# A token-expert table made by matrix products of one-hot keys and stored plainly, in place of element-wise adds into a zeroed table

## The chip, the cores and the metric

The kernel runs on one core of a Trainium2 chip. The metric is the device time of one execution in microseconds (us). Engines are named as the profile names them: PE (TensorE, with PEld for its weight loads), DVE (VectorE), ACT (ScalarE), POOL (GpSimd) and SP (SyncE, which here only issues DMAs). Each engine works off its own queue in order. DMAs run on 16 DMA engines that all queues share.

## The reference

One layer of an encoder, for 1024 tokens of width 1024: a mixing half (attention and a linear recurrence) and a channel half, the PEER mixture of 128 x 128 = 16384 experts. The change touches only the channel half. For each token, 8 heads each choose 16 experts by a pair of keys (i, j), expert number 128 i + j, with softmax weights g:

```python
idx = jnp.take_along_axis(cand_idx, pos, axis=-1)      # 128 experts per token, 16 for each of 8 heads
g = jax.nn.softmax(best, axis=-1)
u = expert_u[idx]
v = expert_v[idx]
act = jax.nn.gelu(jnp.einsum('td,thkd->thk', xt, u))
return jnp.einsum('thk,thkd->td', (g * act).astype(xt.dtype), v)
```

Two heads of a token may choose the same expert; their weights then add up.

## The kernel before

Tokens go in 8 blocks of 128. Blocks 5, 6 and 7 (`GATHER`) fetch the rows of their chosen experts by indirect DMAs. Blocks 0 to 4 (`DENSE`, 640 tokens) are computed against all 16384 experts: 128 groups i of 128 experts each, group i being the experts 128 i + j. For that the weights g of a block stand in a table `d_G` in HBM, one number for each (expert, token), zero where the token did not choose the expert.

**The front.** `run` (L1384) calls `part(0)` and `part(1)`, each for 512 tokens: `attention`, `merge_a`, `lru`, `merge_b`, `ffn_in` (output projection, second norm, then 16 `query` and `score` steps that find each token's best 16 keys with `top16`). Work on the experts' choice is cut into steps in the list `self.steps`, and `pump` (L136) takes some of them at marked places of the stages (`self.rate`). `route(tb)` is the choice of one block, 18 steps on DVE; the places of block 4's routing and of the gathered blocks' are in the dense stage, those of blocks 0 to 3 in `part(1)`.

**The table.** `clear` (L1193) writes zeros over the table with 40 DMAs of 1 MB, one behind each weight load of `part(0)`. `route`'s last step puts the table's addresses `e` and weights `w` into tiles; `gates` (L1163) then issues, for each head and each of its 16 choices, one indirect DMA from POOL (L1174) that adds 128 numbers (one for each token) at 128 addresses in HBM. The 8 heads of a block wait for one another. That is 128 such DMAs a block, 512 for blocks 0 to 3 (`d_G[0]`, 512 tokens = `TE`) and 128 for block 4 (`LATE`, `d_G[1]`), which is routed in the dense stage. In the front they are issued by `pump` through a second rate (9 at most places).

**The dense stage.** `dense` (L1208) runs over the groups. `first(i)` is gelu(u_i h2) as `ps_A`, with operands in two parts (three matmuls for each product); `weigh(i)` multiplies by the table's rows (L1278); every second group `second` adds the product with v into `yac` as `ps_y`. `factors(g)` (L1264) loads the table's rows for two groups, tile `Gt`, one pair ahead; its DMA waits for all adds into that part of the table. Groups 0 to 19 (`KLATE`) work on 512 tokens, groups 20 to 127 on 640; the table part of block 4 is loaded from group 20 on. After the loop, a tail (L1347 on, `ps_Al` and `ps_yl`) computes groups 0 to 19 for block 4. Beside all this `pump` issues the gathers of blocks 5 to 7 (`g_u`, `g_v`: 768 indirect DMAs of 512 KB), first their routing at two steps a place (`FAST`), then at a rate worked out from the number of steps.

The order on each engine comes from a scheduler that takes instructions by their place in the program as their inputs become ready by its own estimate; a tile with a tag has `bufs` buffers and its next use waits for the release of an earlier one.

Of the kernel before, what the change touches and what calls it, by code (L numbers as in the profile page):

```python
# [25 lines left out]
LATE = tuple(b for b in DENSE if b >= S // 256)  # L26
TE = TD - 128 * len(LATE)
KLATE = 20 if LATE else 0
# [26 lines left out]
class Slices:  # L55
# [5 lines left out]
    def tile(self, shape, dt, name):  # L61
        n = int(np.prod(shape[1:]))
        if self.at + n > 1024:
            self.big, self.at = self.pool.tile([128, 1024], F32, tag="t4", bufs=11, name="small"), 0
# [17 lines left out]
class Builder:  # L82
    def __init__(self, ctx, tc, I, out, dbg=None, stop=None):
# [8 lines left out]
        self.rate = dict(unit=((1, 9), (2, 9)), ma=(3, 9), lru=(6, 9), mb=(2, 9), z=(4, 9), q=(2, 9))  # L92
        self.mark, self.heads_of, self.ahead = [], {}, []
        self.adds, self.turn, self.clears, self.due, self.last = {}, None, [], 0.0, None
# [15 lines left out]
    def weight(self, src, cols, scale=None, eng=None):  # L110
# [3 lines left out]
        self.last = nc.sync.dma_start(raw, src)  # L114
        if self.clears:
            self.clears.pop(0)()
# [19 lines left out]
    def pump(self, n, m=0.0):  # L136

        for _ in range(min(n, len(self.steps))):
            self.steps.pop(0)()
        self.due += m  # L140
        while self.due >= 1 and any(q and tb in self.ew for tb, q in self.adds.items()):
            tb = max((tb for tb, q in self.adds.items() if q and tb in self.ew),
                     key=lambda b: (b != self.turn, len(self.adds[b])))
            self.turn = tb
            self.adds[tb].pop(0)()
            self.due -= 1
        self.due = min(self.due, 1.0)
# [37 lines left out]
    def ada(self, g):  # L185
# [4 lines left out]
        def step(dk, h):  # L190
# [4 lines left out]
            w = fp.tile([128, 1024], F32, tag="t4", bufs=11, name="wada")  # L195
# [178 lines left out]
    def head(self, p):  # L374
# [6 lines left out]
        def load():  # L381
            s["x"] = []
            for i in range(4):
                x = fp.tile([128, 1024], F32, tag="t4", bufs=11, name="x")
# [3 lines left out]
        def start():  # L388
            junk = [fp.tile([128, 1024], F32, tag="t4", bufs=11, name="junk") for _ in range(2)]
# [82 lines left out]
    def part(self, p):  # L472
# [9 lines left out]
        if p == 0:  # L482
            self.clears = self.clear()
# [17 lines left out]
    def attention(self, p):  # L501
# [49 lines left out]
        def keys(h, blocks):  # L551
            t = heads.setdefault(h, {})
            if 0 in blocks:
                t["pq"], t["pk"] = self.psum([96, 512], "ps_qT"), self.psum([96, 512], "ps_kT")
                t["q"] = fp.tile([96, 512], F32, tag="t2", name="qT")
                t["k"] = fp.tile([96, 1024], F32, tag="t4", bufs=11, name="kT")
# [58 lines left out]
        for u in range(len(units) + lag + 1):  # L615
# [9 lines left out]
            self.pump(*self.rate["unit"][p])  # L625
# [5 lines left out]
    def softmax(self, p, i, qT, kT, scale):  # L631
# [3 lines left out]
        P = fp.tile([128, 1024], F32, tag="t4", bufs=11, name="P")  # L635
# [54 lines left out]
    def lru(self, p, hs, gb):  # L690
# [7 lines left out]
        def gate(g):  # L698
            t = grp[g] = [fp.tile([128, G, 512], F32, tag="t4", bufs=11, name=nm) for nm in ("ge", "rr", "uu", "bx")]
# [57 lines left out]
        for g in range(8 // G):  # L757
# [5 lines left out]
            self.pump(*self.rate["lru"])  # L763
# [4 lines left out]
        self.pump(*self.rate["lru"])  # L768
# [4 lines left out]
    def merge_a(self, p, hs, attn):  # L773
# [3 lines left out]
        for m in range(8):  # L777
# [9 lines left out]
            self.pump(*self.rate["ma"])  # L787
# [15 lines left out]
    def merge_b(self, p, gb, rec, yf):  # L803
        nc, I, fp = self.nc, self.I, self.fp
        for m in range(8):
# [9 lines left out]
            self.pump(*self.rate["mb"])  # L815
# [12 lines left out]
    def ffn_in(self, p, ys):  # L828
# [3 lines left out]
        for i in range(4):  # L832
            x = fp.tile([128, 1024], F32, tag="t4", bufs=11, name="x1")
# [7 lines left out]
        for cq in range(4):  # L841
# [13 lines left out]
            self.pump(*self.rate["z"])  # L855
# [30 lines left out]
        for i in range(4):  # L886
            if p * 4 + i in DENSE:
                late = p * 4 + i in LATE
                d = DENSE.index(p * 4 + i) * 128 - late * TE
                for j, t in enumerate(h2):  # L890
                    nc.sync.dma_start(self.d_h2T[late][j // 2, :, (j % 2) * 4:(j % 2) * 4 + 4, d:d + 128],
# [5 lines left out]
        st = fp.tile([128, 4, 16, 16], F32, tag="t4", bufs=11, name="st")  # L897
        it = fp.tile([128, 4, 16, 16], U32, tag="t4", bufs=11, name="it")
# [23 lines left out]
        late = [i for i in range(4) if p * 4 + i in GATHER or p * 4 + i in LATE]  # L922
# [5 lines left out]
        for c in range(17):  # L928
# [9 lines left out]
            self.pump(*self.rate["q"])  # L938
# [19 lines left out]
    def route(self, tb):  # L958

        nc = self.nc  # L960
        late = tb in GATHER or tb in LATE
# [20 lines left out]
        def start():  # L982

            if late:
                sit = self.gv([128, 2, 256], F32, "sit")
                self.after((nc.gpsimd if tb in LATE else nc.sync).dma_start(sit, self.d_st[tb]), self.mark)
# [53 lines left out]
        def end():  # L1040
# [15 lines left out]
            else:  # L1056
                pool = self.gp if late else self.fp
                w = pool.tile([128, 128], F32, tag="l_w", bufs=1 if late else TE // 128, name="g_w")
                e = pool.tile([128, 128], I32, tag="l_e", bufs=1 if late else TE // 128, name="g_e")
                nc.vector.tensor_copy(w, W2)  # L1060
                E = t["ij"][:, 0, :]
                nc.vector.scalar_tensor_tensor(E, E, 128.0, t["ij"][:, 1, :], op0=ALU.mult, op1=ALU.add)
                n = TD - TE if late else TE
                nc.vector.tensor_scalar(E, E, float(n), self.cols[:, 99:100], op0=ALU.mult, op1=ALU.add)
                nc.vector.tensor_scalar(e, E, float(DENSE.index(tb) * 128 - late * TE), None, op0=ALU.add)
                self.ew[tb] = e, w
# [96 lines left out]
    def gates(self, tb):  # L1163

        nc = self.nc
        late = tb in LATE
        G = self.d_G[late].rearrange("e (t o) -> (e t) o", o=1)

        def step(h):
            e, w = self.ew[tb]  # L1170
            prev, done = self.heads.get((late, tb), []), []
            others = [o for (l, b), v in self.heads.items() if l == late and b != tb for o in v]
            for s in range(h * 16, h * 16 + 16):
# [34 lines left out]
    def dense(self, da, db):  # L1208
# [119 lines left out]
        if not KLATE:  # L1328
            tokens_in(1, TE, TD)
# [162 lines left out]
```

## Time and profile before

| | us |
|---|---|
| median of 3 runs | 3929.08 (3922.1 to 3934.12) |
| the profiled execution | 3932.46 |
| its span, first to last instruction | 3930.7 |
| PE busy | 3208.3 (82%) |
| DVE busy | 2273.0 (58%) |
| ACT busy | 1105.3 (28%) |
| POOL busy | 2014.3 (51%) |
| DMA queues, share of 16 engines | 35.2% from POOL, 29.7% from SP |

Read by time, not by the shares: the program is a front (0 to about 1316 us), a dense stage (to 3849 us) and a tail. The slices in section 2 of the page show where an engine works; the view of stretches gives its busy time stage by stage; the view of waits says what a stage waited for. PE's clock is granted at 2.4 GHz (1.00) or 1.2 GHz (0.50).

### The profile page before, as it was taken

The numbers are of one execution on the slowest core, as the hardware profiler recorded it, in microseconds if no ns is written. First come the engines' busy times: TensorE is split into PE (matmuls) and PEld (weight loads), VectorE is DVE, ScalarE is ACT, GpSimd is POOL, SyncE is SP. The second block draws the span as 40 slices with busy tenths as digits, with TensorE's granted clock in tenths as the row PEclk, the third lists the DMA queues.
The fourth block names the chain that finished last, engine by engine and source line by source line (L and its number), as shares of the span: only waits on it lengthen the run. The fifth ranks groups of instructions, "written<-read, shape, count | busy, mean of one in ns | idle before, by whom it ended". The sixth has DMA issues, their size and how long they took to land. (4 is left out here: it accounts for less than half of the span.)

```text
span 3930.7 us, 46688 instructions
## 1 busy us (share of the span) xinstructions
PE 3208.3 (82%) x17310; PEld 2582.3 (66%) x17310; DVE 2273.0 (58%) x5192; ACT 1105.3 (28%) x1729; POOL 2014.3 (51%) x1439
## 2 busy tenths in 40 slices
PE   6899989699999500009907999999999999999998
PEld 4577777478688400007706888787888888787776
DVE  6436559883648400009806898677776777674443
ACT  4438343483823100004202222222222222222110
POOL 0000022388888888765774554555554555544440
PEclk9899999799999755559958999999999999999999
DMA  8577452135556322235426888999998999988887
GB/s 326 181 264 248 168 181 75 35 47 92 104 102 142 67 0 0 0 64 142 95 0 217 295 295 299 328 341 330 336 342 319 336 341 343 335 312 310 305 307 260
DMA packets 369212, 814.14 MB, mean 207 GB/s; under 512 B 118404, under 2 KB 157316, under 8 KB 365784
## 3 DMA queue, kind: packets, MB, share of 16 engines
q0 software_dynamic: 203120, 404.38, 35.2%
q1 hardware_dynamic: 165864, 406.78, 29.7%
q8 instruction: 136, 2.23, 0.2%
q14 instruction: 92, 0.75, 0.1%
HBM read 741.47 MB, written 69.55 MB: 206 GB/s over the span
## 5 line engine op out<-in xcount | busy, mean ns | idle before, releaser
L1174 POOL DMA_INDIRECT d_G<-g_w,g_e x640 | 1058.1, 1653 | 337.3 <-issue 203.3
L684 PE MATMUL ps_A<-dh,u 128*128 128x320 f32 (+1 forms) x1888 | 581.0, 321 | 557.0 <-ACT u L101 430.1
L684 PEld LDWEIGHTS ps_A<-dh,u 128*128 128x128 f32 x1888 | 356.6, 189 | 603.0 <-ACT u L101 432.4
L1095 POOL DMA_INDIRECT g_u<-in_expert_u,g_ei x384 | 470.4, 1225 | 401.6 <-PE ps_A L687 127.7
L1125 POOL DMA_INDIRECT g_v<-in_expert_v,g_eT x384 | 435.2, 1133 | 443.5 <-PE g_y L1139 137.4
L1101 DVE CUSTOM_DVE_ANT_0 g_u<-g_u,g_h 128x1024 f32<-128x1024 f32 x384 | 466.1, 1222 | 203.2 <-DMA g_u<-in_expert_u,g_ei 201.6
L685 PE MATMUL ps_A<-dh,u 128*128 128x320 f32 (+1 forms) x1888 | 576.0, 318 | 2.8 <-DMA dh<-d_h2T 2.8
L684 PE MATMUL ps_y<-v,w 128*128 128x512 f32 x1240 | 497.2, 401 | 23.4 <-ACT w L101 12.2
L685 PE MATMUL ps_y<-v,w 128*128 128x512 f32 x1240 | 488.0, 394 | 0.0
L101 ACT CAST v<-raw 128x1024 fp32r<-128x1024 f32 x128 | 134.4, 1050 | 1251.1 <-DMA raw<-in_expert_v 727.1
L1297 DVE TENSOR_TENSOR yac<-yac,ps_y 128x512 f32<-128x512 f32 x610 | 400.7, 683 | 72.6 <-PE ps_y L687 71.4
L687 PE MATMUL ps_y<-v,w 128*128 128x512 f32 x1240 | 391.1, 394 | 3.3 <-DVE w L102 1.4
L1278 DVE TENSOR_TENSOR a<-a,Gt 128x640 f32<-128x640 f32 (+1 forms) x128 | 102.6, 802 | 488.4 <-DMA Gt<-d_G 430.3
L685 PEld LDWEIGHTS ps_A<-dh,u 128*128 128x128 f32 x1888 | 356.9, 189 | 11.8 <-DMA dh<-d_h2T 3.4
L687 PE MATMUL ps_A<-dh,u 128*128 128x320 f32 (+1 forms) x1888 | 328.1, 316 | 0.0
L684 PEld LDWEIGHTS ps_y<-v,w 128*128 128x128 f32 x1240 | 233.9, 189 | 129.4 <-issue 28.5
L687 PEld LDWEIGHTS ps_A<-dh,u 128*128 128x128 f32 x1888 | 292.5, 188 | 6.3
L360 POOL TENSOR_TENSOR hT<-nfull,hT 128x512 fp32r<-128x512 f32 x8 | 10.2, 1288 | 548.7 <-ACT hT L359 548.5
L687 PEld LDWEIGHTS ps_y<-v,w 128*128 128x128 f32 x1240 | 234.3, 189 | 63.4 <-DVE w L102 13.5
L685 PEld LDWEIGHTS ps_y<-v,w 128*128 128x128 f32 x1240 | 234.5, 189 | 44.8
L102 DVE TENSOR_TENSOR v<-raw,v 128x1024 fp32r<-128x1024 f32 x128 | 156.3, 1221 | 165.7 <-ACT v L101 165.7
L102 DVE TENSOR_TENSOR whl<-wraw,whl 128x1024 fp32r<-128x1024 f32 (+2 forms) x136 | 155.7, 1146 | 155.7 <-ACT whl L101 155.6
(355 smaller groups left out, 5498.1 us busy)
## 6 DMA issues: line engine op xcount, KB each, us to landing
raw<-in_uT SPq DMA_DIRECT2D x128, 512.0 KB, 5.6
raw<-in_expert_v SPq DMA_DIRECT2D x128, 512.0 KB, 6.8
d_G<-zero SPq DMA_DIRECT2D x40, 1024.0 KB, 8.3
wraw<-in_w_in SPq DMA_DIRECT2D x64, 512.0 KB, 3.6
Gt<-d_G SPq DMA_DIRECT2D x64, 512.0 KB, 7.1
wada<-in_w_ada SPq DMA_DIRECT2D x32, 512.0 KB, 9.3
wraw<-in_w_query SPq DMA_DIRECT2D x32, 512.0 KB, 4.9
d_G<-g_w,g_e POOLq DMA_INDIRECT x640, 3.0
```

The source lines that it names most:

```text
L101: self.nc.scalar.copy(hi, src)
L102: (eng or self.nc.vector).tensor_tensor(lo, src, b32(hi), op=ALU.subtract)
L360: (eng or nc.vector).tensor_tensor(lo, full, b32(hi), op=ALU.subtract)
L684: nc.tensor.matmul(ps, lh, rh, start=(n == 0), stop=False)
L685: nc.tensor.matmul(ps, lh, rl, start=False, stop=False)
L687: st = nc.tensor.matmul(ps, ll, rh, start=False, stop=(n == len(terms) - 1))
L1095: st = nc.gpsimd.indirect_dma_start(out=u[:], out_offset=None, in_=I["expert_u"], in_offset=bass.IndirectOffsetOnAxis(ap=g["ei"][:, s:s + ...
L1101: nc.vector.tensor_tensor_reduce(out=u, in0=u, in1=g["h2"], scale=1.0, scalar=0.0, op0=ALU.mult, op1=ALU.add, accum_out=g["act"][:, s:s + 1])
L1125: st = nc.gpsimd.indirect_dma_start(out=v[:], out_offset=None, in_=I["expert_v"], in_offset=bass.IndirectOffsetOnAxis(ap=g["eT"][:, t:t + ...
L1174: st = nc.gpsimd.indirect_dma_start(out=G, out_offset=bass.IndirectOffsetOnAxis(ap=e[:, s:s + 1], axis=0), in_=w[:, s:s + 1], in_offset=No ...
L1278: nc.vector.tensor_tensor(a, a, Gs[g][:, m, :], op=ALU.mult)
L1297: nc.vector.tensor_tensor(yac[tb][:, ds], yac[tb][:, ds], ps, op=ALU.add)
```

## The change

`clear`, `gates`, the zero tile, `e` and `w`, the second rate of `pump` and the whole treatment of block 4 as a late block (`LATE`, `TE`, `KLATE`, the tail) go. `route(4)` moves into `part(1)`. The table becomes `d_G[c, j, i, t]`: token chunk c of `GC` = 32 tokens, then key j, key i and the token in its chunk. `table(tb)` makes a block's part of it in 33 steps. The first transposes the block's i, j and g (three 128 x 128 transposes on PE, one ACT copy `ch`), so that a token's 128 choices lie on the partitions. Each further step is for four tokens: `oneB` (one DVE instruction) compares the iota 0..127 with the choices' j, `oneA` (one DVE instruction for each token) compares it with i and multiplies by g; four fp32 matmuls `ps_G` give, for each token, the sum over the choices, a [j, i] matrix that is the table's part for that token; two ACT copies put it into the tiles `gs`, token innermost. After 8 steps two SP DMAs of 1 MB store 32 tokens; `gs` has two buffers, so the next 8 steps' copies wait for these stores. Where the program had `gates` now stands `table`: `pump` takes its steps from the one list, and what is left when `part(1)` is over runs before the dense stage. The tag `t4` has 9 buffers in place of 11.

```diff
-LATE = tuple(b for b in DENSE if b >= S // 256)
-TE = TD - 128 * len(LATE)
-KLATE = 20 if LATE else 0
+GC = 32
...
-        self.rate = dict(unit=((1, 9), (2, 9)), ma=(3, 9), lru=(6, 9), mb=(2, 9), z=(4, 9), q=(2, 9))
+        self.rate = dict(unit=(1, 2), ma=3, lru=6, mb=2, z=4, q=2)
...
-        self.last = nc.sync.dma_start(raw, src)
-        if self.clears:
-            self.clears.pop(0)()
+        nc.sync.dma_start(raw, src)
...
-                self.ew[tb] = e, w
+                self.chosen = t["ij"], W2
...
+    def table(self, tb):
+        nc, fp = self.nc, self.fp
+        t = {}
+        def start():
+            ij, W = self.chosen
+            pt = self.psum([128, 3, 128], "ps_ch")
+            for k, x in enumerate((ij[:, 0, :], ij[:, 1, :], W)):
+                nc.tensor.transpose(pt[:, k, :], x, self.ident)
+            t["ch"] = fp.tile([128, 3, 128], F32, tag="ch", bufs=1, name="ch")
+            nc.scalar.copy(t["ch"], pt)
+        def step(q):
+            ch = t["ch"]
+            if q % (GC // 4) == 0:
+                t["st"] = [fp.tile([128, 64, GC], F32, tag="gs", bufs=2, name="gs") for _ in range(2)]
+            B = fp.tile([128, 4, 128], F32, tag="t2", name="oneB")
+            A = fp.tile([128, 4, 128], F32, tag="t2", name="oneA")
+            iota = self.iota
+            nc.vector.tensor_tensor(B, iota[:, None, :].to_broadcast([128, 4, 128]),
+                                    ch[:, 1, q * 4:q * 4 + 4, None].to_broadcast([128, 4, 128]), op=ALU.is_equal)
+            for m in range(4):
+                n = q * 4 + m
+                nc.vector.tensor_scalar(A[:, m, :], iota, ch[:, 0, n:n + 1], ch[:, 2, n:n + 1], op0=ALU.is_equal,
+                                        op1=ALU.mult)
+            ps = self.psum([128, 4, 128], "ps_G")
+            for m in range(4):
+                nc.tensor.matmul(ps[:, m, :], B[:, m, :], A[:, m, :], start=True, stop=True)
+            k = q % (GC // 4) * 4
+            for m in range(2):
+                nc.scalar.copy(t["st"][m][:, :, k:k + 4].rearrange("p i t -> p t i"), ps[:, :, m * 64:(m + 1) * 64])
+            if q % (GC // 4) == GC // 4 - 1:
+                c = DENSE.index(tb) * (128 // GC) + q // (GC // 4)
+                for m in range(2):
+                    nc.sync.dma_start(self.d_G[c, :, m * 64:(m + 1) * 64, :], t["st"][m])
+        return [start] + [lambda q=q: step(q) for q in range(32)]
...
-        points = (128 * 2 + len(groups) * NB + KLATE) * RATE
+        points = (128 * 2 + len(groups) * NB) * RATE
...
         def factors(g):
...
-            Gs[g] = da.tile([128, hi - lo, n], F32, tag="G", bufs=2, name="Gt")
-            for k, (p0, p1) in enumerate(((0, TE), (TE, n))):
...
+            Gs[g] = da.tile([128, TD // GC, hi - lo, GC], F32, tag="G", bufs=2, name="Gt")
+            nc.sync.dma_start(Gs[g].rearrange("j c i t -> j c (i t)"),
+                              self.d_G[:, :, lo:hi, :].rearrange("c j i t -> j c (i t)"))
...
-        for k, tb in enumerate(LATE):
...
                 for tb in range(p * 4, p * 4 + 4):
-                    if tb in DENSE and tb not in LATE:
-                        self.steps += self.soon[tb] if tb in self.soon else self.route(tb)[0]
-                        self.adds[tb] = self.gates(tb)
-            self.pump(1 << 30, 1 << 30)
+                    if tb in DENSE:
+                        self.steps += (self.soon[tb] if tb in self.soon else self.route(tb)[0]) + self.table(tb)
+            self.pump(1 << 30)
...
-            for tb in LATE:
-                self.steps += self.route(tb)[0] + self.gates(tb)
```

PE's queue in `merge_a` of `part(1)`, between the two projections of one output chunk and those of the next. Before:

```order
L685 MATMUL ps_pa<-attnl,whl 128x512
L687 MATMUL ps_pa<-attnh,whl 128x512 x4
L684 MATMUL ps_ga<-hT,whl 128x512
L685 MATMUL ps_ga<-hT,whl 128x512
L684 MATMUL ps_ga<-hT,whl 128x512
```

The same place now:

```order
L670 MATMUL ps_pa<-attnl,whl 128x512
L672 MATMUL ps_pa<-attnh,whl 128x512 x4
L1169 MATMUL ps_G<-oneA,oneB 128x128 x9
L669 MATMUL ps_ga<-hT,whl 128x512
L1169 MATMUL ps_G<-oneA,oneB 128x128 x3
L670 MATMUL ps_ga<-hT,whl 128x512
```

Three steps' matmuls, 12, now stand between the projections, and the queue passes them only when DVE has made their one-hots. Counted over the whole queue, the 640 matmuls of `ps_G` stand so: 177 within `part(1)`'s attention, 79 in `merge_a`, 40 in `lru`, 88 in `merge_b`, and 256 from the query steps on.

DVE's queue where `part(1)` ends and the dense stage begins (`u` is the split of the first expert weights, `a` the first use of the table). Before:

```order
L951 MATCH_REPLACE wk<-st,sc 128x128
L102 TENSOR_TENSOR u<-raw,u 128x1024
L952 MAX st<-wk 128x8
L953 MAX_INDEX it<-st,wk 128x8
L102 TENSOR_TENSOR u<-raw,u 128x1024
L1278 TENSOR_TENSOR a<-a,Gt 128x512
```

Now, after 29 steps of the same two rows:

```order
L1161 TENSOR_TENSOR oneB<-cst,ch 128x512
L1165 TENSOR_SCALAR oneA<-cst,ch 128x128 x4
L1161 TENSOR_TENSOR oneB<-cst,ch 128x512
L1165 TENSOR_SCALAR oneA<-cst,ch 128x128 x4
L1161 TENSOR_TENSOR oneB<-cst,ch 128x512
L1165 TENSOR_SCALAR oneA<-cst,ch 128x128 x4
L99 TENSOR_TENSOR u<-raw,u 128x1024 x2
L99 TENSOR_TENSOR v<-raw,v 128x1024
L99 TENSOR_TENSOR u<-raw,u 128x1024
L1248 TENSOR_TENSOR a<-a,Gt 128x640
```

All 32 steps of block 4 stand at the end of the front, behind the last of its routing, and the split of the first `u` comes after them.

SP's queue at the same place. Before:

```order
L1241 DMA raw<-in_uT 128x1024
L1323 DMA dh_11528<-d_h2T_95 128x4x512
L1323 DMA dh_11529<-d_h2T_95 128x4x512
L1323 DMA dh_11537<-d_h2T_95 128x4x512
L1323 DMA dh_11531<-d_h2T_95 128x4x512
L1241 DMA raw<-in_uT 128x1024
L1268 DMA Gt<-d_G_97 128x2x512
L1241 DMA raw<-in_expert_v 128x1024
```

Now:

```order
L1292 DMA dh_13387<-d_h2T 128x2560
L1176 DMA d_G<-gs 128x2048 x2
L1216 DMA raw<-in_uT 128x1024
L1176 DMA d_G<-gs 128x2048 x6
L1216 DMA raw<-in_expert_v 128x1024
L1216 DMA raw<-in_uT 128x1024
L1239 DMA Gt<-d_G 128x20x64
L970 DMA sit<-d_st 128x512
L1239 DMA Gt<-d_G 128x20x64
```

The stores of block 4's table stand on the same queue as the dense stage's loads, ahead of the first `Gt`; and a `Gt` load is now 128 x 20 pieces of 64 numbers (256 bytes) where it was 128 x 2 pieces of 512 and later 128 x 2 more of 128.

## Rows read from the trace of the kernel before

**Rows 1.** The page's 40 slices of 98 us: busy tenths, PE's granted clock.

```profile
PE   6899989699999500009907999999999999999998
POOL 0000022388888888765774554555554555544440
PEclk9899999799999755559958999999999999999999
```

**Rows 2.** Waits, one line each: who waited for whom, us, times, longest.

```profile
DVE a L1278 <- DMA Gt<-d_G: 430.3, 1, 430.3
PE ps_A L684 <- DVE yac L1297: 125.6, 3, 124.6
```

**Rows 3.** Stretches: length, busy us of PE, PEld, DVE, ACT, POOL, clock, DMA share, GB/s.

```profile
726.00:887.00 161.00, 150.53 (x876) 111.31 (x877) 131.07 (x553) 117.12 (x257) 119.75 (x72) 0.90 0.29 39
887.00:1151.00 264.00, 257.05 (x1088) 204.98 (x1087) 124.97 (x161) 136.62 (x167) 224.35 (x131) 0.99 0.53 102
1211.50:1316.00 104.50, 102.84 (x516) 86.34 (x514) 100.82 (x494) 36.60 (x55) 88.94 (x52) 1.00 0.59 130
1333.00:1762.00 429.00, 0.49 (x3) 0.20 (x2) 2.73 (x4) 2.86 (x4) 340.57 (x223) 0.50 0.24 10
1762.00:1960.00 198.00, 194.69 (x842) 158.44 (x842) 185.76 (x517) 72.08 (x91) 129.41 (x69) 0.99 0.54 129
1960.00:2085.00 125.00, 0.37 (x3) 0.11 (x1) 1.98 (x3) 2.09 (x2) 92.01 (x60) 0.52 0.23 10
2085.00:3849.00 1764.00, 1738.51 (x10035) 1418.88 (x10036) 1230.12 (x1817) 382.76 (x546) 905.55 (x768) 0.99 0.89 318
3849.00:3931.00 82.00, 71.06 (x402) 50.96 (x401) 17.35 (x31) 5.54 (x20) 0.00 (x0) 0.97 0.77 281
```

**Rows 4.** The use of the table, by its line: durations, first and last start.

```profile
L1278 DVE TENSOR_TENSOR a<-a,Gt x128: 669/821/886, 1756.8 to 3833.0; 128x640 f32<-128x640 f32 x108, 128x512 f32<-128x512 f32 x20
```

**Rows 5.** Groups of instructions in the front, shapes apart: busy us, mean ns, idle before.

```profile
L736 DVE TENSOR_TENSOR bx<-ig,xc 128x512 f32<-128x512 f32 x16 | 11.0, 687 | 36.3 <-ACT ig L734 36.3
L661 DVE TENSOR_SCALAR P<-P,sm 128x128 f32<-128x128 f32 x8 | 2.3, 282 | 0.1
L588 ACT COPY PT<-ps_pT 128x256 f32<-128x256 f32 x16 | 6.0, 375 | 10.2 <-PE ps_pT L586 10.2
```

**Rows 6.** Order of time in the query steps, DVE and PE: start us, us, instruction.

```profile
1285.52 0.27 DVE L952 MAX8 st<-wk 128x8 f32<-128x128 f32 x1
1285.71 0.28 DVE L949 MAX8 st<-sc 128x8 f32<-128x128 f32 x1
1255.05 1.05 PE L915 MATMUL ps_sc<-sk,qrT 128*128 128x128 f32 x8
1255.86 0.48 PE L684 MATMUL ps_qr<-h2T,whl 128*128 128x512 f32 x1
```

**Rows 7.** The stretch 682 to 887, instructions on routing tiles alone (`rM`, then `eq`).

```profile
682.00:887.00 205.00, 0.00 (x0) 0.00 (x0) 47.58 (x276) 1.26 (x4) 0.87 0.26 42
682.00:887.00 205.00, 42.41 (x48) 0.87 0.26 42
```

**Rows 8.** DMA issues: KB each, median us from issue to landing.

```profile
Gt<-d_G SPq DMA_DIRECT2D x64, 512.0 KB, 7.1
d_hT<-hT SPq DMA_DIRECT2D x8, 1024.0 KB, 3.9
```

**Rows 9.** The stretch 2600 to 3500, instructions on `ps_A` alone, then on `ps_y`.

```profile
2600.00:3500.00 900.00, 403.55 (x2688) 395.71 (x2688) 46.44 (x112) 1.00 0.92 336
2600.00:3500.00 900.00, 402.69 (x1687) 311.25 (x1688) 181.39 (x280) 0.00 (x0) 1.00 0.92 336
```

**Rows 10.** DMA packets of one queue in 1288.2:1292, 1400:1700 and 2624.5:2625.

```profile
q1 hardware_dynamic: 144, 0.07, 6.0%
...
q0 software_dynamic: 22608, 0.09, 22.1%
...
q1 hardware_dynamic: 76, 0.16, 83.9%
```

More of the change, by code (lines that the diff above doesn't have):

```diff
@@ L134, in rsqrt, with pump @@
         return y
-    def pump(self, n, m=0.0):
+    def pump(self, n):
         for _ in range(min(n, len(self.steps))):
             self.steps.pop(0)()
[L140 to L147, printed above, removed]
     def show(self, name, ap):
@@ L624, in attention @@
                 mixes.pop(u - lag - 1)()
-            self.pump(*self.rate["unit"][p])
+            self.pump(self.rate["unit"][p])
         if p == 0:
@@ L762, in lru @@
                 scan(g - 1)
-            self.pump(*self.rate["lru"])
+            self.pump(self.rate["lru"])
         for m in range(G):
@@ L767, in lru @@
         scan(8 // G - 1)
-        self.pump(*self.rate["lru"])
+        self.pump(self.rate["lru"])
         if p == 1:
@@ L920, in score @@
                 self.top16(sc[:, i, :], w2, st[:, i, c, :], it[:, i, c, :])
-        late = [i for i in range(4) if p * 4 + i in GATHER or p * 4 + i in LATE]
+        late = [i for i in range(4) if p * 4 + i in GATHER]
         for i in range(4):
@@ L1160, in finish @@
         nc.sync.dma_start(self.out[tb * 128:(tb + 1) * 128, :], gr)
[L1163 to L1173, printed above, removed]
-                st = nc.gpsimd.indirect_dma_start(
-                    out=G, out_offset=bass.IndirectOffsetOnAxis(ap=e[:, s:s + 1], axis=0),
-                    in_=w[:, s:s + 1], in_offset=None, compute_op=ALU.add)
-                for o in done:
-                    self.tc.declare_no_dep(st.ins, o, reason="the experts of a head are distinct")
-                for o in others:
-                    self.tc.declare_no_dep(st.ins, o, reason="the columns of two blocks are distinct")
-                self.after(st, prev)
-                done.append(st.ins)
-            self.heads[late, tb] = done
-        return [lambda h=h: step(h) for h in range(8)]
+    def table(self, tb):
[32 more added lines that the diff above has]
+        return [start] + [lambda q=q: step(q) for q in range(32)]
@@ L1226, in pump @@
             self.mark = [st.ins]
-        def tokens(i):
-            return TE if i < KLATE else TD
         started = set()
@@ L1283, in second @@
             lo, hi = groups[g]
-            for tb in range(tokens(lo) // 128):
+            for tb in range(NB):
                 cs = slice(tb * 128, (tb + 1) * 128)
```

140 lines of the change are left out of this document (33 added, 107 removed).

## The prediction

> **What bounds the kernel now.** I read the slices first [rows 1]. POOL works from slice 6 on; PE is at 9 tenths nearly everywhere, but shows two holes, slices 15 to 18 and 21, with its clock at 0.5. The view of waits names them [rows 2]: DVE's first use of the table waits 430.3 us for the load `Gt`, and PE waits 124.6 us behind DVE at group 20, where block 4's part of the table is first used. Both loads wait for POOL's adds into HBM. The view of stretches confirms it [rows 3]: from 1333 to 1762 and from 1960 to 2085 PE works 0.5 and 0.4 us while POOL is busy. So 554 us are a wait for the way the table is made. Everywhere else the stages are full: in `merge_a`, `lru` and `merge_b` (887 to 1151) PE is busy 257.05 of 264 us, in the query steps (1211.5 to 1316) PE and DVE both about 101 of 104.5, in the dense stage PE 1738.51 of 1764 with DMA at 0.89. New work in the front therefore isn't free, and that is the sum to make.
>
> The program falls at one point: the first use of the table, `weigh(0)`, starts at 1756.8 [rows 4]. I work out when it starts now, and then what follows it (3930.7 - 1756.8 = 2173.9 us).
>
> **Price of a step of `table`** (four tokens, 160 steps in all). On DVE one instruction 128x512 and four 128x128 with two per-partition scalars; the nearest rows are 687 and 282 ns [rows 5], together 1.815 us, an upper end. Back to back, an instruction starts before the one ahead has ended (0.27 long, the next 0.19 later, [rows 6]), some 85 ns each: 1.39 us, which I take. On PE four fp32 matmuls 128x128: the same four in a score step (x8, two records for each) take 1.05 us, and the next matmul starts 0.81 after [rows 6]; I take 0.9 a step. On ACT two copies of 128x256 at 375 ns [rows 5]: 0.75.
>
> **Front.** Counted by PE's queue, 44 steps stand in the attention, 52 in `merge_a` to `merge_b`, 64 (blocks 3 and 4) from the query steps on.
> Attention: PE 150.5 + 44 x 0.9 = 190 us against 161 now, +29 if it filled every gap, +40 at today's idle 10.5 us. DVE would have 131 - 44 (the routing of two of the four blocks leaves: 47.58 + 42.41 us for four, [rows 7], so 22 a block) + 61 = 148, ACT 117 + 33: neither is the bound. +40, bounds 25 and 60 (each step at DVE's price).
> `merge_a` to `merge_b`: PE alone gives 52 x 0.9 = +47. PE meets the matmuls in queue order, three steps in a clump in `merge_a`, and waits if DVE is late; if it waited each time, 52 x 1.815 = +94. DVE's load is 125 + 44 + 72 = 241 us in a stretch of 311, so it is mostly in time: a third of the way, +62.
> `z` to the normalised transpose: +3.
> Query steps: DVE is the bound: 32 steps of block 3 are 45 us, half of block 4's routing 12: +58, bounds 54 and 70.
> Then everything that `pump` has left: the rest of block 4's routing, 14 us of chained DVE work, 32 steps (45 us, 58 at the upper price), the last copies, a store (1 MB lands in 3.9 us, [rows 8]) and the first `Gt` (7.1): 16 more. +75, bounds 62 (routing hidden) and 95 (58, and PE at its low clock because it idles, as in the holes of [rows 1]). Nothing can cover this: the dense stage needs the whole table.
> `weigh(0)`: 1316 (end of the query steps) + 40 + 62 + 3 + 58 + 75 = **1554**, 203 earlier than now; bounds 1504 and 1640.
>
> **Dense stage.** From 2173.9: the second hole goes, -125 [rows 2]. The tail of groups 0 to 19 for block 4, 82 us from 3849 on [rows 3], goes except for some 12 us of last sums and stores: -70. In its place 20 groups work on 640 tokens instead of 512: a group costs PE 403.55/56 = 7.21 us for `ps_A` and 402.69/56 = 7.19 for `ps_y` [rows 9], so a fifth of 14.4, 2.9 x 20 = +58. The clearing stores and POOL's adds cost nothing on the path outside the holes. The routing of blocks 5 to 7 stays in the first ten groups, where DVE was busy 185.76 of 198 us [rows 3] with 512 tokens; at 640 it is over full: +12.
> The load `Gt`: 16 + 16 pieces on each DMA engine before, 160 of 256 bytes now. Three prices of a piece are in the trace [rows 10] (busy share x time x 16 engines / packets): 512 bytes in 1288.2 to 1292 took 28 ns, 2048 bytes about 88, and an add of 4 bytes (a read and a write) 46.9. Before, a load cost 16 x 88 + 16 x 28.5 = 1.86 us of every engine. No row shows 256 bytes: half of 28.5 is 14 (2.3 us a load), the add's price is 47 (7.5 us). I take about 21, between the first two, since these too are plain reads: +1.5 us for each pair of groups. A pair takes 2 x 900/56 = 32.1 us with DMA at 0.92 [rows 9], so 2.5 us are free, and the load is one pair ahead. But more pieces take longer to get past the gathers' pieces (landing 15 to 28 us instead of 7.1, my estimate from five times the pieces), and weight loads stand behind on SP's queue. +20, bounds 0 and 165.
> Sum: 2173.9 - 125 - 70 + 58 + 12 + 20 = 2069. With `weigh(0)` at 1554 the span is 3623, and 1.8 us lie outside it: 3625 against 3932.46 of the profiled execution, -308. That execution is 3.4 above the median, so **3620**.
>
> The rows give 512 bytes 28 ns and 2048 bytes 88 [rows 10]: a piece costs nearly by its bytes. The Trainium skill (DMA: Bandwidth & Descriptors, Specifications) names 512 bytes as the least transfer for line rate, and the layout that this change gives the table is below that. By this rule a 256-byte piece would cost as much as one of 512, 4.6 us a load, 2.7 more than before; against 2.5 us free that adds some 10 us in all, which is within my +20. If it cost twice as much, it is the first rival. No run here shows pieces of 256 bytes.
>
> **Rivals.**
> *DMA becomes the bound of the dense stage.* At the add's 47 ns a load costs 5.6 us more, 3.1 over what is free, in some 54 pairs: +165 in place of +20, 3765. For it: DMA at 0.92, PE's queue without reserve, gathers and weights sharing the engines. Against: these are reads, and 512 bytes took 28 ns.
> *The steps run one after another.* If PE waits in full for the one-hots of each of the 96 steps that stand among PE's own work, each costs 1.815 + 1.05 = 2.87 us instead of the 102/96 = 1.06 taken: +173, 3790. For it: clumps of three steps in `merge_a`. Against: DVE's queue is free to run ahead by some buffers, and its load fits.
> *A light front.* Steps at the lower bounds everywhere (25 + 47 + 54 + 62, `weigh(0)` at 1504) and pieces that cost nothing: 3620 - 50 - 20 = 3550.
> *Slower than before.* It has one place: `Gt` in the dense stage, if a small piece is far dearer than I take. What I count as gained, 308 + 20 = 328 us, over 64 loads is 5.1 us each; with the 2.5 free and the 1.86 of now a load would have to keep every engine 9.5 us, 59 ns a piece. From there on the change loses; at 65 ns it is 3620 - 20 + 64 x (10.4 - 1.86 - 2.5) = 3985. The nearest row is 46.9, of an operation that does more.
> *It doesn't do what it says*: the dense stage still waits for the table, because SP's queue stores 20 MB of it just ahead. Of 16 x 1 MB for block 4 only the last pair is late; this is in the 16 us above.
>
> **How the numbers follow.** The forecast's case 0.65 (3570 to 3700), DMA as the bound 0.14, steps one after another 0.07, a light front 0.09, slower 0.04, and 0.01 for a cancellation near zero. Measured times of this kernel tell 0.3%, 12 us, from no change. The range reaches from the light front to the DMA rival: 3550 to 3770; left out are the serial steps, the slower case and the edges. Faster 0.95, same 0.01, slower 0.04.
>
> **What would show it.** The holes of [rows 1] gone, and `weigh(0)` near 1554; if it is there by 1500, the one-hots are cheaper than rows 5 and 6 say, if after 1640, PE waits for them. The instructions `oneB` and `oneA` sum to about 1.4 us a step, `ps_G` to 0.9. Query steps and what follows them last about 240 us. In the dense stage groups stand 16.1 us apart as now; with DMA as the bound the spacing rises to 17.6, the DMA share goes to 0.98 and PE's `ps_A` or DVE's `a` waits for weights or `Gt`. The tail `ps_Al` is gone, and the span ends some 12 us after the last group. The forecast fails if pieces cost over 40 ns, or if the 32 steps at the end of the front take over 100 us.

## The result

The changed kernel takes 3799.58 us (median of 4 runs, 3796.31 to 3811.1) against 3926.32 for the kernel before: a ratio of 0.968, with a 95% interval of 0.9654 to 0.9706. It is faster, as forecast, but by 127 us and not by the 308 of the sum, and the time lies above the whole range (3550 to 3770).

The page of the changed kernel, its slices (now 95 us each), for [rows 1]:

```profile
PE   6899989689988966569988999999999999999997
POOL 0000013000000000000144445555555555444400
PEclk8899999799999987779999999999999999999998
```

Both holes are gone, and so is nearly all of POOL's work in the front. In their place there is a shallow dip in slices 15 to 18: PE at 5 and 6 tenths, its clock at 0.7 to 0.8. The use of the table, for [rows 4] (line, count, durations in ns, first and last start):

```profile
L1248 DVE TENSOR_TENSOR a<-a,Gt x128: 794/821/887, 1735.1 to 3772.5; 128x640 f32<-128x640 f32 x128
```

`weigh(0)` starts at 1735.1; the forecast had 1554, the kernel before 1756.8. From there to the end are 3809.3 - 1735.1 = 2074 us; the forecast had 2069. So the whole miss, 181 us, lies ahead of the dense stage. The stretches of the changed kernel, for [rows 3] (length, busy PE, PEld, DVE, ACT, POOL, clock, DMA share, GB/s): attention, merges with the recurrence, query steps, what follows them, groups 0 to 19, the other groups, the end.

```profile
727.00:956.00 229.00, 197.21 (x1217) 152.85 (x1218) 172.65 (x643) 158.87 (x339) 0.00 (x0) 0.93 0.22 79
956.00:1300.00 344.00, 314.37 (x1506) 259.36 (x1505) 232.30 (x521) 192.93 (x278) 0.00 (x0) 0.96 0.34 117
1370.00:1641.00 271.00, 173.88 (x746) 149.12 (x745) 154.08 (x711) 64.71 (x110) 0.00 (x0) 0.79 0.18 62
1641.00:1735.00 94.00, 61.21 (x387) 54.69 (x387) 80.87 (x255) 43.04 (x81) 1.75 (x2) 0.85 0.57 210
1735.00:2024.00 289.00, 273.02 (x1489) 244.59 (x1488) 252.53 (x560) 84.50 (x119) 73.41 (x58) 0.98 0.65 207
2024.00:3772.00 1748.00, 1706.58 (x9880) 1390.95 (x9880) 1156.12 (x1686) 376.55 (x536) 813.57 (x710) 1.00 0.87 300
3772.00:3809.00 37.00, 13.93 (x60) 10.73 (x59) 20.03 (x22) 1.17 (x2) 0.00 (x0) 0.73 0.36 128
```

The query steps stand out. They took 104.5 us with PE and DVE both full [rows 3]; now they take 271, and neither engine is full: PE 174, DVE 154. An engine that is the bound is busy; here nobody is, so the two wait for each other. The view of waits over 1372 to 1641 says so:

```profile
PE ps_G L1169 <- DVE oneA L1165: 97.1, 21, 7.3
DVE st L933 <- ACT sc L901: 97.0, 12, 8.9
```

And the order of time shows one turn of it (start, us, what; in brackets the idle time before and who ended it):

```profile
1451.67 1.05 PE L899 MATMUL ps_sc<-sk,qrT 128*128 128x128 f32 x8
...
1453.30 0.59 ACT L901 COPY sc<-ps_sc 128x512 f32<-128x512 f32 x1
1453.92 0.49 DVE L933 MAX8 st<-sc 128x8 f32<-128x128 f32 x2 [8.47 <-ACT sc L901]
...
1458.14 0.34 DVE L1165 TENSOR_SCALAR oneA<-cst,ch 128x128 f32<-128x128 f32 x1
...
1458.63 4.13 PE L1169 MATMUL ps_G<-oneA,oneB 128*128 128x128 f32 x16 [5.90 <-DVE oneA L1165]
...
1462.41 0.77 PE L669 MATMUL ps_qr<-h2T,whl 128*128 128x512 f32 x1
...
1469.05 1.05 PE L899 MATMUL ps_sc<-sk,qrT 128*128 128x128 f32 x8
```

Read it as a ring. PE makes the scores (`ps_sc`, 1451.67). ACT copies them. DVE, idle for 8.47 us, starts the choice at 1453.92, and only when that is nearly done comes the one-hot that PE's next instruction needs (1458.14). PE, idle for 5.90 us, does two steps of the table, then the next projection `ps_qr` (1462.41), then the next scores (1469.05), for which DVE has begun to wait. One turn is 17.4 us: 2.3 to the scores' arrival, 4.7 to the one-hots, 3.8 of `ps_G`, 6.6 of projection. Sixteen turns are 278 us, and the stage lasts 271. Before, the same projection, scores and choice overlapped, 6.5 us for a query step.

### The profile page after: what moved, and what is told of

Same layout as the page of the kernel before. It is cut to its first block, busy times and chain, and to the rows that moved or that the text cites. A ratio compares the mean times of both kernels' runs of the same rounds, so it can differ in the third digit from the quotient of the medians.

```text
span 3809.3 us, 50002 instructions
## 1 busy us (share of the span) xinstructions
PE 3427.5 (90%) x18805; PEld 2810.2 (74%) x18805; DVE 2543.8 (67%) x5976; ACT 1271.9 (33%) x2054; POOL 938.1 (25%) x798
## 5 line engine op out<-in xcount | busy, mean ns | idle before, releaser
L669 PE MATMUL ps_A<-dh,u 128*128 128x320 f32 x2048 | 609.7, 311 | 5.2 <-DVE yac L1267 5.2
L1070 POOL DMA_INDIRECT g_u<-in_expert_u,g_ei x384 | 453.7, 1181 | 620.3 <-DMA raw<-in_uT 218.1
L670 PE MATMUL ps_A<-dh,u 128*128 128x320 f32 x2048 | 605.9, 309 | 0.0
L669 PE MATMUL ps_y<-v,w 128*128 128x512 f32 x1280 | 515.7, 403 | 49.5 <-DVE yac L1267 40.4
L670 PE MATMUL ps_y<-v,w 128*128 128x512 f32 x1280 | 504.4, 394 | 0.1
L1267 DVE TENSOR_TENSOR yac<-yac,ps_y 128x512 f32<-128x512 f32 x630 | 414.1, 682 | 95.5 <-PE ps_y L672 94.2
L669 PEld LDWEIGHTS ps_A<-dh,u 128*128 128x128 f32 x2048 | 385.3, 188 | 38.2 <-issue 20.1
L672 PE MATMUL ps_y<-v,w 128*128 128x512 f32 x1280 | 402.9, 394 | 2.2 <-DVE w L99 0.7
L670 PEld LDWEIGHTS ps_A<-dh,u 128*128 128x128 f32 x2048 | 385.5, 188 | 1.8
L1169 PE MATMUL ps_G<-oneA,oneB 128*128 128x128 f32 x1280 | 226.0, 329 | 160.1 <-DVE oneA L1165 148.3
L669 PEld LDWEIGHTS ps_y<-v,w 128*128 128x128 f32 x1280 | 242.4, 189 | 168.7 <-DVE yac L1267 64.6
L672 PE MATMUL ps_A<-dh,u 128*128 128x320 f32 x2048 | 343.2, 310 | 0.0
L1169 PEld LDWEIGHTS ps_G<-oneA,oneB 128*128 128x128 f32 x1280 | 202.0, 230 | 191.4 <-issue 123.2
L672 PEld LDWEIGHTS ps_A<-dh,u 128*128 128x128 f32 x2048 | 312.4, 189 | 0.0
L672 PEld LDWEIGHTS ps_y<-v,w 128*128 128x128 f32 x1280 | 242.3, 189 | 62.2 <-DVE w L99 10.0
L670 PEld LDWEIGHTS ps_y<-v,w 128*128 128x128 f32 x1280 | 242.6, 190 | 46.2 <-DVE v L99 0.5
L1172 ACT COPY gs<-ps_G 128x256 f32<-128x256 f32 x320 | 167.6, 641 | 219.5 <-PE ps_G L1169 193.9
```

Source lines behind the costliest of these rows:

```text
L669: nc.tensor.matmul(ps, lh, rh, start=(n == 0), stop=False)
L670: nc.tensor.matmul(ps, lh, rl, start=False, stop=False)
L672: st = nc.tensor.matmul(ps, ll, rh, start=False, stop=(n == len(terms) - 1))
L1070: st = nc.gpsimd.indirect_dma_start(out=u[:], out_offset=None, in_=I["expert_u"], in_offset=bass.IndirectOffsetOnAxis(ap=g["ei"][:, s:s + ...
L1169: nc.tensor.matmul(ps[:, m, :], B[:, m, :], A[:, m, :], start=True, stop=True)
L1172: nc.scalar.copy(t["st"][m][:, :, k:k + 4].rearrange("p i t -> p t i"), ps[:, :, m * 64:(m + 1) * 64])
```

## The experiments

Three questions: is it this ring; which link closes it; and what do the steps cost once it is open? The theory is that PE's `ps_G`, standing ahead of the next projection in PE's queue and reading one-hots that stand behind the choice in DVE's queue, closes the ring. Against it stood two rivals: that the steps are simply dear, wherever they stand; and that the ring closes through the split of the next query weights (`whl`), which also stands behind the one-hots on DVE.

**No steps in the query stage.**

```diff
-        self.rate = dict(unit=(1, 2), ma=3, lru=6, mb=2, z=4, q=2)
+        self.rate = dict(unit=(1, 2), ma=3, lru=6, mb=2, z=4, q=0)
```

> No step of the table is taken at the query steps' places; the 64 steps of blocks 3 and 4 and block 4's routing all run after them, and nothing else is changed. Theory (loop): in the changed kernel the query stage lasts 269 us, with DVE idle 97 us for the scores and PE idle 97 us for the one-hots, because PE's table matmuls stand ahead of the next projection and wait for one-hots that DVE makes only behind the choice from the last scores. Then the query stage falls back to 105 to 112 us, what follows it grows from 92 to about 92 + 32 x 1.63 + 12 = 156, the first use of the table comes at about 1637 and the time is about 3700. Rival (load): the steps cost the same wherever they stand, 5 us each in this part of the program; the time stays within 15 us of 3800.

Measured: 3690.73 us, ratio to the kernel before 0.9401 (0.9376 to 0.9427). Query stage and what follows it, in its stretches:

```profile
1358.60:1460.50 101.90, 101.90 (x514) 86.50 (x513) 100.28 (x483) 34.12 (x52) 0.00 (x0) 1.00 0.32 106
1460.50:1613.30 152.80, 94.36 (x622) 83.55 (x621) 140.97 (x494) 71.95 (x141) 1.75 (x2) 0.88 0.45 171
```

The stage is back at 102 us with PE full at 1.00, and 64 steps in a row behind it cost 153, with DVE busy 141 of them. The same work takes 110 us less for standing elsewhere. The rival "dear wherever they stand" is out.

**The matmuls two steps behind their one-hots.** Nothing is left out; a step now issues the matmuls, copies and stores of two steps before.

```diff
+        def mats(q):
+            A, B = t.pop(q)
...
+        def both(q):
+            if q >= 2:
+                mats(q - 2)
+            if q < 32:
+                step(q)
-        return [start] + [lambda q=q: step(q) for q in range(32)]
+        return [start] + [lambda q=q: both(q) for q in range(32 + 2)]
```

> The same instructions, but a step's four matmuls, copies and stores are issued two steps behind its one-hots. Theory (loop, closed by PE's table matmuls): PE finds the one-hots ready, the query stage falls from 269 to 165 to 185 us (DVE's 152 busy plus little), the time to about 3710; attention and the merges gain some 20 us as well. Rival 1 (loop, closed by the split of the next query weights, which stands behind the one-hots on DVE): the query stage stays above 230. Rival 2 (load): unchanged, 3800 within 15.

Measured: 3634.56 us, ratio 0.9241 (0.9225 to 0.9256). That is 165 us below the changed kernel, and the expected 3710 was 75 too high. Its attention, query stage and what follows that, by stretches:

```profile
722.90:911.40 188.50, 178.15 (x1192) 142.35 (x1193) 157.55 (x571) 151.80 (x333) 0.00 (x0) 0.95 0.24 88
1301.00:1455.40 154.40, 135.75 (x686) 113.01 (x683) 148.04 (x660) 56.53 (x94) 0.00 (x0) 0.96 0.30 101
1455.40:1566.00 110.60, 71.39 (x454) 63.83 (x453) 97.88 (x323) 51.39 (x99) 1.75 (x2) 0.88 0.52 197
```

and the same two waits as above, in its query stage:

```profile
PE ps_G L1173 <- DVE oneA L1163: 14.6, 16, 4.1
...
DVE st L933 <- ACT sc L901: 6.3, 5, 1.9
```

97.1 us became 14.6 and 97.0 became 6.3; DVE is busy 148 of 154. PE's queue in the query stage reads alike by names in both kernels; this is the changed one:

```order
L899 MATMUL ps_sc<-sk,qrT 128x128 x4
L1169 MATMUL ps_G<-oneA,oneB 128x128 x5
L669 MATMUL ps_qr<-h2T,whl 128x512
L1169 MATMUL ps_G<-oneA,oneB 128x128 x3
L670 MATMUL ps_qr<-h2T,whl 128x512
```

What differs is which one-hots the eight `ps_G` read: there those that DVE makes behind the choice from the scores of one turn before, here those that it made a turn earlier.

One more thing differs: each block's list of steps is two items longer, so fewer steps stand in the query stage and more behind it. The instructions on `ps_G` in the query stage (PE, PEld and ACT; eight records of PE make a step), in the changed kernel and then with the delay:

```profile
1370.00:1641.00 271.00, 61.05 (x232) 53.35 (x232) 31.29 (x58) 0.79 0.18 62
1301.00:1455.40 154.40, 32.65 (x168) 26.74 (x168) 22.22 (x41) 0.96 0.30 101
```

29 steps became 21. The fair measure is the stage together with what follows it, 64 steps in both kernels: 271 + 94 = 365 us became 154 + 111 = 265. By the stretches the rest of the gain is the attention's (229 to 188.5), the merges' (344 to 322) and 2 us of the output projection; the expectation had only some 20 us for attention and merges.

**The split of the query weights on POOL.**

```diff
-            wt = self.weight(I["w_query"][c], 1024, eng=nc.gpsimd if p == 0 else None)
+            wt = self.weight(I["w_query"][c], 1024, eng=nc.gpsimd)
```

> The query weights' low half (16 instructions of 1.2 us on DVE) is made by POOL in part(1) too, as it is in part(0); the table's steps are untouched. Theory (loop closed by PE's table matmuls): only DVE's load falls, by 16 x 1.2 = 19 us, so 3780, the query stage at 250. Rival 1 (loop closed by the split): the query stage falls to 165 to 185, 3710. Rival 2 (load): 3780 as well.

Measured: 3816.99 us, ratio 0.9702 (0.9679 to 0.9725), no gain at all. The waits of its query stage:

```profile
DVE st L933 <- ACT sc L901: 129.5, 14, 9.8
...
PE ps_G L1169 <- DVE oneA L1165: 100.5, 21, 12.6
```

The stage takes 277 us. The rival link is out. Nor did the expected 19 us come: what DVE saves in a ring it spends waiting (129.5 us for 97.0).

**Both edits together** (those of the two experiments above).

> Both edits of the two experiments ahead. Theory: whichever of the two links closes the loop, it is open now; the query stage lasts 140 to 165 us, bounded by DVE's work (132 us without the splits), and the time is about 3690. Rival (load): 3780.

Measured: 3641.51 us, ratio 0.9257 (0.924 to 0.9274): the same as with the matmuls later alone. The query stage falls from 154 to 149 us, within the 140 to 165 expected; the time of 3690 was set too high.

**One step instead of two** (the same edit with 1 for 2).

> The matmuls one step behind their one-hots instead of two or none. A query place takes two steps; with one step's delay the first group of matmuls finds its one-hots made at the place before, the second still waits for this place's first one-hots. Theory (loop closed by the last wait): PE then still waits at each place, for one step's one-hots less: the query stage lies between 154 and 271 us, near 210 to 245, the time near 3700 to 3750. If the gain of two steps had come from another cause than the wait (fewer buffers held, other order in the merges), one step would give nearly all of it: 3640 to 3660.

Measured: 3715.58 us, ratio 0.9445 (0.9412 to 0.9478), as the theory had it. Its query stage, by stretch and by waits:

```profile
1324.20:1549.00 224.80, 155.81 (x718) 132.71 (x717) 156.10 (x708) 59.59 (x102) 0.00 (x0) 0.84 0.24 81
```

```profile
PE ps_G L1173 <- DVE oneA L1163: 68.4, 13, 7.4
DVE st L933 <- ACT sc L901: 68.3, 12, 7.1
```

With a delay of 0, 1 and 2 steps the stage lasts 271, 225 and 154 us, and PE's wait is 97, 68 and 15. It holds 29, 25 and 21 steps; together with what follows it, 64 steps each time, it takes 365, 323 and 265 us. In the attention one step of delay already gives nearly everything (229, 195, 188). Its places take two items as well, so the theory doesn't say why one step is enough there, and no run shows it.

**PE's part alone** (the one-hots left out, so the table holds other numbers).

```diff
-            nc.vector.tensor_tensor(B, iota[:, None, :].to_broadcast([128, 4, 128]),
-                                    ch[:, 1, q * 4:q * 4 + 4, None].to_broadcast([128, 4, 128]), op=ALU.is_equal)
-                nc.vector.tensor_scalar(A[:, m, :], iota, ch[:, 0, n:n + 1], ch[:, 2, n:n + 1], op0=ALU.is_equal,
-                                        op1=ALU.mult)
...
-                nc.tensor.matmul(ps[:, m, :], B[:, m, :], A[:, m, :], start=True, stop=True)
+                nc.tensor.matmul(ps[:, m, :], ch[:, 0, :], ch[:, 2, :], start=True, stop=True)
```

> DVE's one-hots are left out (the table's matmuls take the transposed choices themselves as operands, so the table holds other numbers); matmuls, copies and stores stay where they are. Theory (the loop between DVE and PE): without DVE in it there is none; the query stage lasts 104.5 + 32 x 0.9, 130 to 145 us, attention about 190, and what follows the queries about 65 with the copies as its bound. First use of the table near 1520. Rival (PE's own load, matmuls at the low clock): the query stage stays over 200.

**DVE's part alone** (the matmuls left out; the copies take the one-hots).

```diff
-            ps = self.psum([128, 4, 128], "ps_G")
-                nc.tensor.matmul(ps[:, m, :], B[:, m, :], A[:, m, :], start=True, stop=True)
...
-                nc.scalar.copy(t["st"][m][:, :, k:k + 4].rearrange("p i t -> p t i"), ps[:, :, m * 64:(m + 1) * 64])
+                nc.scalar.copy(t["st"][m][:, :, k:k + 4].rearrange("p i t -> p t i"), (B, A)[m][:, :, 0:64])
```

> The table's matmuls are left out; the one-hots are made as before and the copies take them directly (so the table holds other numbers). PE no longer waits for DVE. Theory (loop): DVE's load alone, 152 us of work in the query stage, gives 150 to 170 there; attention 161 to 175, merges 264 to 280; first use of the table near 1490. Rival (DVE's load or its order alone is too much): the query stage stays over 220 although PE takes no part.

One execution each, 3564.98 and 3604.08 us. Query stage of PE's part alone, then, from the other kernel, of DVE's alone:

```profile
1294.30:1424.00 129.70, 128.37 (x750) 112.69 (x749) 107.04 (x547) 63.03 (x111) 0.00 (x0) 1.00 0.38 128
```

```profile
1267.10:1434.50 167.40, 119.53 (x517) 95.95 (x516) 147.72 (x679) 66.27 (x108) 0.00 (x0) 0.85 0.29 99
```

130 us and 167 us: each half of the added work fits. `weigh(0)` starts at 1500.5 and 1532.5, against 1735.1 with both in the changed order and 1565.8 with both and two steps of delay. So neither load makes the 271 us; the coupling does. (For PE the expected 1520 was 20 us too late; for DVE 1490 was too early, since its merges and its attention grew more than expected, to 292 and 180 us.)

**Pieces of 128 bytes.**

```diff
-GC = 32
+GC = 16
```

> Chunks of 16 tokens instead of 32, so a load of the table's rows is 320 pieces of 128 bytes on each DMA engine instead of 160 of 256. If a small piece has a fixed price near the 21 ns that the prediction took, a load takes 3.4 us more of every engine and the dense stage grows by up to 215 us; at 14 ns by 140; if a piece costs by its bytes, the dense stage stays within 30 us of 2074. The front: unchanged within 15 us.

One execution, 3856.16 us. The dense stage takes 3854.0 - 1731.3 = 2123 us, 49 more than with 256 bytes: between "by its bytes" (within 30) and a fixed price of 14 ns (140). The first twenty groups take 290 us, 289 with 256 bytes; the growth is in the later ones. The price can be estimated from SP's queue in 2600 to 3500. First the kernel before, then the changed one, then this one (packets, MB, share of 16 engines):

```profile
q1 hardware_dynamic: 31774, 78.62, 24.6%
```

```profile
q1 hardware_dynamic: 85973, 76.99, 27.8%
```

```profile
q1 hardware_dynamic: 149253, 74.25, 31.4%
```

Before: 24.6% of 900 is 221 us on each engine; 28 loads `Gt` at 1.86 are 52, and 115 transfers of 512 KB the rest, 1.47 each, which is taken for the other two kernels as well. Changed: 250 us less 114 x 1.47 leaves 82 for 27 loads, 3.05 each, 19 ns a piece. With 128 bytes: 283 less 109 x 1.47 leaves 122 for 26 loads, 4.7 each, 14.7 ns a piece.

**More steps ahead of the queries.** With the matmuls two steps later, other numbers of items at the places:

```diff
-        self.rate = dict(unit=(1, 2), ma=3, lru=6, mb=2, z=4, q=2)
+        self.rate = dict(unit=(1, 2), ma=3, lru=9, mb=4, z=8, q=0)
```

> On top of the matmuls two steps later: more steps at the places of the recurrence, the second merge and the output projection (9, 4 and 8 instead of 6, 2 and 4) and none in the query steps, so that block 3's table is done before the queries and only block 4's is left behind them. Theory: a step costs about 1 us in the merges, where PE bounds and DVE has room, against 1.6 behind the queries and more in them; merges and output projection grow by 30 to 40, the query stage falls from 154 to 105, the rest stays at about 105: first use at about 1555, 3615 to 3630. If the steps in the merges cost 1.6 as well, no change against 3635.

Measured: 3635.81 us, ratio 0.9245 (0.9217 to 0.9273): no change against 3634.56. From the end of the attention to the first query step it now takes 445 us for 389, with 32 steps more there: 56/32 = 1.7 us a step. The 1 us of the expectation was wrong; its alternative held.

**None in the query stage** (the delay of two, and q=0).

> Matmuls two steps later, and no steps at the query steps' places: 64 steps behind the queries. Theory: the query stage falls from 154 to 103 us, what follows it rises from 110 to about 110 + 32 x 1.63 = 162 less the routing that moves with it; first use of the table at 1560 to 1570, 3625 to 3640: once the loop is open, a step costs about DVE's 1.6 us inside the query stage or behind it.

Measured: 3644.53 us, ratio 0.9254 (0.9222 to 0.9286). Query stage 101.9 us, behind it 159.7, `weigh(0)` at 1564.4 against 1565.8. Both stretches together take 262 us for 265, so with the ring open a step costs the same in the query stage as behind it. The time is a little above the 3625 to 3640 expected.

**More, then most, in the attention** (the delay of two and these rates).

```diff
+        self.rate = dict(unit=(1, 3), ma=4, lru=6, mb=3, z=2, q=0)
```

> Matmuls two steps later; three places' items instead of two in the attention, 4 and 3 instead of 3 and 2 in the merges, 2 instead of 4 in the output projection, none in the query steps. By PE's queue 63 steps stand in the attention instead of 41, 32 behind the queries instead of 43. Theory: in the attention a step costs 0.7 to 0.9 us (DVE has 157 of 188 us to do there, PE 178), so +18, behind the queries 11 steps less and none in the query stage: -50 there and +10 in the merges; first use near 1535 to 1550, 3605 to 3620. If DVE becomes the bound of the attention: +36 there, 3625 or more.

Measured: 3624.33 us, ratio 0.921 (0.9173 to 0.9247). `weigh(0)` came at 1545.6 as expected; the attention grew from 188.5 to 219.3, 31 us for 22 steps: 1.4 a step, more than the 0.7 to 0.9 of the theory, less than 1.6. The time lies between the 3605 to 3620 expected and the 3625 of the alternative. It is the lowest median of all, but its interval overlaps that of the delay alone.

```diff
+        self.rate = dict(unit=(1, 4), ma=3, lru=3, mb=2, z=1, q=0)
```

> As before with four items in the attention, where 85 steps then stand. DVE would have 157 + 44 x 1.6 = 227 us there less the routing's share: it becomes the bound, the attention grows by 35 to 45 against that of 188; merges fall by 10 to 15. First use near 1530 to 1560, 3600 to 3630: within 0.5% of the variant with three.

Measured: 3657.14 us, ratio 0.9295 (0.9257 to 0.9333). Its attention:

```profile
726.10:999.70 273.60, 241.90 (x1568) 197.59 (x1569) 247.76 (x879) 195.84 (x424) 0.00 (x0) 0.91 0.28 107
```

PE 242 and DVE 248 of 274: 85 us more than with 41 steps, not 35 to 45, and `weigh(0)` at 1587.1, not 1530 to 1560. Here both engines are near their bound; that work handed between them then overlaps less well is a guess that no run tests.

## Why the prediction was wrong

**What held.** The holes went, and the dense stage came out as summed: 2074 us for 2069. The first twenty groups with the hole fell from 348 us (1756.8 to 2105.2) to 289, -60 where the terms -125, +58 and +12 gave -55. The end fell from 97.7 us to 36.8, -61 for -70. The remaining groups grew by 21 us, the forecast for the small pieces was +20; the terms were not measured one by one. A piece of 256 bytes costs 19 ns by the estimate above; 21 were taken. The Trainium skill (DMA: Bandwidth & Descriptors, Specifications) names 512 bytes as the least transfer for line rate. The traces agree in part: in bytes per time, 256 at 19 ns is slower than 512 at 28.5 [rows 10], but a piece of 256 is not as dear as one of 512, and one of 128 is cheaper still.

**A step cost a sixth more than was taken.** The steps in the front, by group (busy us, mean ns, idle before):

```profile
L1169 PE MATMUL ps_G<-oneA,oneB 128*128 128x128 f32 x1280 | 226.0, 329 | 160.1 <-DVE oneA L1165 148.3 <-ACT P L639 3.0 <-DVE carry L736 2.2
...
L1165 DVE TENSOR_SCALAR oneA<-cst,ch 128x128 f32<-128x128 f32 x640 | 182.1, 338 | 0.0
L1172 ACT COPY gs<-ps_G 128x256 f32<-128x256 f32 x320 | 167.6, 641 | 219.5 <-PE ps_G L1169 193.9 <-DMA d_G<-gs 23.0 <-issue 2.1
L1161 DVE TENSOR_TENSOR oneB<-cst,ch 128x512 f32<-128x512 f32 x160 | 109.0, 681 | 1.3 <-ACT ch L1152 1.3
```

`oneB` is as its row said (681 for 687), `oneA` takes 338 ns and not 282, and back to back behind the queries a step comes every 1.63 us, for 1.39. On ACT a copy takes 641 and not 375. PE was busy 226.0/160 = 1.41 us a step, for 0.9; with PE's part alone, where the granted clock was 1.00, the query stage's 29 steps added (128.4 - 102.8)/29 = 0.88 each, so 0.9 was the price at the high clock. What follows the queries came out at 94 us for 75. Only 7 of these 19 are the price of a step: the 32 steps of block 4 took 52 us for 45 (1667.7 to 1719.8), the rest of the routing with the last steps of block 3 27 for 14, the end 15 for 16.

**The step that failed is the one on the query stage**: "DVE is the bound: 32 steps of block 3 are 45 us, half of block 4's routing 12: +58, bounds 54 and 70". It added loads engine by engine and took the larger. This was nearly right for the work: with the delay of two, the stage and what follows it take 265 us, and the sum had 104.5 + 58 + 75 = 237. It was wrong for the order. PE's queue and DVE's queue were already coupled once in a query step, scores to choice; `ps_G` behind the one-hots added the way back, and with both ways in one turn the engines work in turns. The stage came out 271 - 162 = 109 us over the sum, of the 181; of the 128 by which it and what follows it missed together, the delay takes back 100. The prediction's own sign held: "if after 1640, PE waits for them".

**The attention missed in the same way, in small.** Forecast +40 with bounds 25 and 60, measured +68. With the delay it is +28: "neither is the bound" was right. Of the 40 us that go, PE's rows show 21 as waits (12 ahead of `ps_G`, 9 ahead of `ps_o`) and 15 as `ps_G` busy longer (54.0 us for 38.5, 42 steps for 39). The merges took +80 for +62 (+58 with the delay); `z` and the transposes +9 for +3. Together 28 + 18 + 6 + 109 + 19 = 180 of the 181.

**The rival was at hand, in the wrong place.** "The steps run one after another" gave 3790, and 3799.58 is near it. But it put the wait among the 96 steps in the attention and the merges, at 2.87 us each, and excused it because "DVE's queue is free to run ahead by some buffers". In the query stage DVE is not free to run ahead: what stands ahead of the one-hots in its queue waits for PE. There a step costs (271 - 104.5)/30 = 5.6 us, by the 30 whose one-hots are made in the stage; among the 96 it was (68 + 80)/96 = 1.5, not 2.87. The parts of the order that stand ahead of the prediction are from `merge_a` and from the end of the front; the query stage, where the ring is, was summed without a look at both queues together. So the agreement of 3790 with the result is partly chance, and the chance of 0.07 given to it was too low.

**Smaller slips.** Block 4's table is stored by 8 transfers of 1 MB and the whole table is 40 MB; the prediction's last rival says 16 and 20. No term of the sum used these counts. All stores of the table together held ACT's copies up for 23.0 us (the group of `gs` above). The 28 ns of a 512-byte piece are the queue's time shared among 128 pieces; by all 144 packets, as the prediction's formula has it, they would be 25.

**Whether the forecast's time was possible**: yes. With one edit that only delays the matmuls by two steps the kernel takes 3634.56 us, and `weigh(0)` starts at 1565.8, 12 us from the 1554 of the sum.

## What to carry to other kernels

Work that is added to two engines may fit each of them (130 and 167 us here) and still make a stage far longer (271), if it makes a ring: engine A waits in its queue for something that stands, in B's queue, behind what waits for A. So look at the order of both queues over one turn of the loop, not only at busy shares; a stage in which both engines are less busy than the stage is long, and wait for each other by equal amounts (97.1 and 97.0 us here), is the sign. The cure isn't less work but distance: let the consumer take what was made one turn earlier, by as many steps as one turn makes (two here; one gave 42 of 100 us). Moving the steps out of the loop served as well here: 255 us for the two stretches, against 265.

## What the runs showed of the hardware

An ACT copy from PSUM of 128x256 numbers took 641 ns where it writes every 32nd number of a row, 626 where every 16th, and 375 where it writes them side by side [rows 5]. The stride is the difference that the code shows; no run tests it alone.

The wait goes with a lower clock, which lengthens the ring: in the query stage PE was granted 0.79 of 2.4 GHz on average, 1.00 where nothing stood between the projections. In the turn shown above, PE stands still and then works on at 0.50:

```profile
1453.90:1458.60 4.70, 0.00 (x0) 0.00 (x1) 4.68 (x31) 0.00 (x0) 0.00 (x0) 0.92 0.03 7
1462.40:1464.60 2.20, 2.20 (x7) 1.80 (x7) 0.06 (x1) 0.00 (x0) 0.00 (x0) 0.50 1.02 417
```

The first projection matmuls behind the table's take 0.77 and 0.63 us, later ones in the same turn 0.39. Over the whole stage PE's 746 records are busy 173.9 us; with PE's part alone, at 1.00, 750 are busy 128.4. So some 45 us of the stage, an estimate, are the low clock and not the wait itself.

Reads in small pieces cost 28.5, 19 and 14.7 ns for 512, 256 and 128 bytes (the last two by the estimates above), so halving a piece saves a third and then a quarter of its time. An estimate from the last two: some 10 ns of a piece do not depend on its size.
